# Cross entropy over 8192 rows: 128 loads of 16000 columns became 125 loads of 16384 columns that run across row ends

## The chip, the cores and the metric

The kernel runs on one core of a Trainium2 chip. In the profile's words ACT is the Scalar engine, DVE the Vector engine, POOL GpSimd, and SP the engine that issues the loads. The DMA engines carry data from HBM, the chip's memory, to SBUF, the core's own memory. The metric is the device time of one execution in microseconds (us). The experiments were run in four batches on different chips, each with runs of the kernel before in the same rounds; unless it says otherwise, a difference is taken against those. The profile's span is about 1.7 us shorter than the device time of the same execution; I compare device times with device times and spans with spans.

## The reference, cut to what matters

```python
# logits: (16, 512, 32000) float32, labels: (16, 512) integer
logits_max = np.max(logits, axis=-1, keepdims=True)
log_sum_exp = np.log(np.sum(np.exp(logits - logits_max), axis=-1)) + logits_max.squeeze(-1)
loss = log_sum_exp - logits[label of the row]        # shortened
```

There are 8192 rows of 32000 float32 values, 1048.58 MB, each read once. The output has 8192 numbers. The kernel leaves the maximum out: the data are normal draws, so exp does not overflow.

## The kernel before

Each of the 128 partitions owns 64 consecutive rows, which stand as one contiguous run of 64 x 32000 values in HBM. Three SBUF buffers of 16000 columns take the loads in turn. ACT computes exp in place and sums as it goes (`accum_out`). 64 indirect gathers on POOL, one for each row of a partition, fetch the labels' logits. A tail of shrinking loads keeps the work after the last landing short.

```python
W = 16000
lg_pg = lg.rearrange("(p g) v -> p g v", g=G)          # P = 128, G = 64, V = 32000
...
plan(0, [[4000, 4000, 8000], [16000]], [(0, 0), (0, 1), (0, 2), (1, 0)])
for g in range(1, G - 2):
    plan(g, [[W], [W]], [(0, 0), (1, 0)])
plan(G - 2, [[W], [10000, 6000]], [(0, 0), (1, 0), (1, 1)])
plan(G - 1, [[7400, 5840, 2260], [4540, 3720, 2920, 1780, 1460, 1120], [960]], ...)
...
data = ctx.enter_context(tc.tile_pool(name="data", bufs=3))
sums = persist.tile([P, G - 1, 5], FP32)
...
for g in range(G):
    nc.gpsimd.indirect_dma_start(out=lab_logit[:, g:g + 1], ..., in_=lg,
        in_offset=bass.IndirectOffsetOnAxis(ap=idx[:, g:g + 1], axis=1))
...
def exp(g, ap):
    ...
    nc.scalar.activation(out=ap, in_=ap, func=EXP, accum_out=s)

for j, (g, b, at, n) in enumerate(loads):
    ...
    nc.sync.dma_start(out=t[:, at:at + n], in_=lg_pg[:, g, c0:c0 + n])
    exp(g, t[:, at:at + n])
```

The softmax here doesn't subtract the row's maximum and nothing guards it: scores larger than these inputs give would overflow.

## Time and profile before

| | before |
|---|---|
| device time | 2435.71 us median of 3 (2435.50 to 2435.98) |
| bytes read | 1048.67 MB, 431 GB/s over the span |
| ACT busy | 72% of the span |
| loads, exps | 139, 139 |
| one full load, steady | 18.90 us (three in 56.70 us) |
| exp of one full load | 13.54 us |

These lines are from the page of the kernel before. The engine line has busy time, share of the span and instructions. The DMA line has the busy tenths of the 16 DMA engines in 40 equal slices. The queue lines have packets, MB and share of the engines' time. The last line is the chain that ended last.

```profile
span 2434.1 us, 807 instructions
DVE 1.3 (0%) x5; ACT 1748.9 (72%) x281; POOL 61.0 (3%) x70
DMA  9999999999999999999999999999999999999998
...
q1 hardware_dynamic: 20304, 1048.62, 99.8%
...
q14 instruction: 6, 0.05, 0.0%
...
DMA t<-in_logits_dram 76%; ACT t L105 24%; SPq L113 0%; ACTq L105 0%; ACT logsum_last L127 0%; DVE res_last L128 0%; ACT logsum L120 0%
```

The DMA engines are full from end to end. The chain's 24% of ACT does not mean that ACT holds up a quarter of the time. The same chain in order of time (start, duration, what) shows why:

```profile
1137.65 42.97 DMA t<-in_logits_dram
...
1180.70 13.64 ACT t L105 x2
1194.35 43.65 DMA t<-in_logits_dram
...
1238.08 13.64 ACT t L105 x2
1251.73 42.96 DMA t<-in_logits_dram
...
1294.78 13.64 ACT t L105 x2
```

With three buffers, the end of an exp releases the load three places later, and that load lands behind two others that were already queued. The step "exp 13.64, DMA 42.96" is therefore three loads long: 56.70 us for three loads of 8.192 MB, 18.90 us each, 433.4 GB/s. The Trainium skill, "DMA: Bandwidth & Descriptors", section "Where 436 GB/s comes from", puts the ceiling of the SBUF ports at 435.2 GB/s, and this trace comes to 99.6% of it.

The groups by shape (busy us, mean ns | idle before, releaser) give the price of an exp: 0.833 ns per column from the two shapes, and about 0.20 us that does not depend on the width.

```profile
L105 ACT ACTIVATE t<-t 128x16000 f32<-128x16000 f32 x124 | 1678.5, 13536 | 666.4 <-DMA t<-in_logits_dram 666.4
...
L105 ACT ACTIVATE t<-t 128x8000 f32<-128x8000 f32 x1 | 6.9, 6869 | 6.4 <-DMA t<-in_logits_dram 6.4
```

### The profile page before, as it was taken

To read this page: it belongs to the slowest core of one execution; us is meant where nothing else is said; L and a number is where in the kernel's file an instruction comes from. 1 tells how busy PE (TensorE), PEld (TensorE's weight loads), DVE (VectorE), ACT (ScalarE), POOL (GpSimd) and SP (SyncE) were. 2 spreads that over 40 slices of the span, in tenths; PEclk is the share of its full clock that TensorE was granted. 3 is DMA by queue.
4 is the path that set the end of the run, shared out by engine and by line. 5 is a ranking of instruction groups with operands and counts; after the bars stand their busy time and mean duration, and the time that the engine had idled before them with its cause. 6 is when DMAs were issued, how large, how long until landed. Compare 5 with 4: busy or idle time off the path is not lost.

```text
span 2434.1 us, 807 instructions
## 1 busy us (share of the span) xinstructions
DVE 1.3 (0%) x5; ACT 1748.9 (72%) x281; POOL 61.0 (3%) x70
## 2 busy tenths in 40 slices
DVE  0000000000000000000000000000000000000000
ACT  4777766777677776777677776777667776777769
POOL 3222000000000000000000000000000000000000
DMA  9999999999999999999999999999999999999998
GB/s 421 422 421 433 425 438 431 427 438 438 433 426 436 438 434 426 435 438 434 426 435 436 435 430 431 436 435 430 431 436 438 431 427 436 438 433 426 438 433 377
DMA packets 22502, 1048.77 MB, mean 431 GB/s; under 512 B 4576, under 2 KB 4704, under 8 KB 5216
## 3 DMA queue, kind: packets, MB, share of 16 engines
q1 hardware_dynamic: 20304, 1048.62, 99.8%
q0 software_dynamic: 2048, 0.04, 0.1%
q10 hardware_dynamic: 144, 0.07, 0.0%
q14 instruction: 6, 0.05, 0.0%
HBM read 1048.67 MB, written 0.03 MB: 431 GB/s over the span
## 4 chain that ended last, share of the span: by engine, by line
DMA 76%; ACT 24%; issue 0%; SPq 0%; ACTq 0%; DVE 0%
DMA t<-in_logits_dram 76%; ACT t L105 24%; SPq L113 0%; ACTq L105 0%; ACT logsum_last L127 0%; DVE res_last L128 0%; ACT logsum L120 0%
## 5 line engine op out<-in xcount | busy, mean ns | idle before, releaser
L105 ACT ACTIVATE t<-t 128x16000 f32<-128x16000 f32 (+5 forms) x139 | 1734.8, 12481 | 681.4 <-DMA t<-in_logits_dram 681.2
L89 POOL DMA_INDIRECT lab_logit<-in_logits_dram,idx x64 | 60.3, 942 | 178.3 <-DMA lab_logit<-in_logits_dram,idx 174.5
L105 ACT ACTIVATION_READ_ACCUMULATOR t<-t 128x1 f32 x139 | 25.9, 186 | 0.0
L84 ACT ACT_TABLE_LOAD x1 | 1.3, 1283 | 1.2 <-PEq L144 1.2
L118 DVE TENSOR_REDUCE totals<-sums 128x63 f32<-128x315 f32 x1 | 0.5, 480 | 2398.9 <-ACT t L105 2398.9
L87 POOL TENSOR_TENSOR idx<-idx,labs 128x64 int32<-128x64 int32 x1 | 0.3, 322 | 7.5 <-DMA labs<-in_labels_dram 7.5
L85 DVE MEMSET sums<- 128x315 f32 x1 | 0.3, 321 | 0.9 <-PEq L144 0.9
L127 ACT ACTIVATE logsum_last<-sums_last,part 128x1 f32<-128x1 f32 x1 | 0.3, 294 | 0.0
L121 DVE TENSOR_TENSOR res<-logsum,lab_logit 128x63 f32<-128x63 f32 x1 | 0.2, 225 | 25.3 <-ACT logsum L120 25.3
L120 ACT ACTIVATE logsum<-totals 128x63 f32<-128x63 f32 x1 | 0.2, 238 | 0.0
L86 POOL IOTA idx<- 128x64 int32 x1 | 0.2, 172 | 0.4 <-PEq L155 0.4
L123 DVE TENSOR_REDUCE part<-sums_last 128x1 f32<-128x9 f32 x1 | 0.2, 163 | 4.0 <-ACT t L105 4.0
L128 DVE TENSOR_TENSOR res_last<-logsum_last,lab_logit 128x1 f32<-128x1 f32 x1 | 0.2, 159 | 1.2 <-ACT logsum_last L127 1.2
L144 POOL MEMSET const-uint8-127<- 128x1 uint8 x1 | 0.1, 118 | 0.0
L144 POOL MEMSET const-bfloat16-1.0<- 128x1 bf16 x1 | 0.1, 113 | 0.0
L144 POOL MEMSET const-float32-0.0<- 128x1 f32 x1 | 0.1, 98 | 0.2 <-issue 0.2
L144 POOL MEMSET const-float32-1.0<- 128x1 f32 x1 | 0.1, 104 | 0.0
## 6 DMA issues: line engine op xcount, KB each, us to landing
t<-in_logits_dram SPq DMA_DIRECT2D x124, 8000.0 KB, 43.0
t<-in_logits_dram SPq DMA_DIRECT2D x1, 5000.0 KB, 35.9
t<-in_logits_dram SPq DMA_DIRECT2D x2, 2000.0 KB, 9.6
t<-in_logits_dram SPq DMA_DIRECT2D x1, 4000.0 KB, 21.4
t<-in_logits_dram SPq DMA_DIRECT2D x1, 3700.0 KB, 32.9
t<-in_logits_dram SPq DMA_DIRECT2D x1, 3000.0 KB, 42.6
t<-in_logits_dram SPq DMA_DIRECT2D x1, 2920.0 KB, 39.5
t<-in_logits_dram SPq DMA_DIRECT2D x1, 2270.0 KB, 26.4
```

Source lines behind the costliest of these rows:

```text
L84: nc.scalar.preload_act_table_set("natural_log_exp_and_others")
L85: nc.vector.memset(sums[:], 0.0)
L86: nc.gpsimd.iota(idx[:], pattern=[[V, G]], base=0, channel_multiplier=G * V)
L87: nc.gpsimd.tensor_tensor(out=idx[:], in0=idx[:], in1=labs32, op=ALU.add)
L89: nc.gpsimd.indirect_dma_start(out=lab_logit[:, g:g + 1], out_offset=None, in_=lg, in_offset=bass.IndirectOffsetOnAxis(ap=idx[:, g:g + 1], ...
L105: nc.scalar.activation(out=ap, in_=ap, func=EXP, accum_out=s)
L118: nc.vector.reduce_sum(out=totals[:], in_=sums[:], axis=X)
L120: nc.scalar.activation(out=logsum[:], in_=totals[:], func=LN)
L121: nc.vector.tensor_tensor(out=res[:], in0=logsum[:], in1=lab_logit[:, 0:G - 1], op=ALU.subtract)
L123: nc.vector.reduce_sum(out=part[:], in_=sums_last[:, 0:K - 1], axis=X)
L127: nc.scalar.activation(out=logsum_last[:], in_=sums_last[:, K - 1:K], func=LN, bias=part[:])
L144: nc = _bacc.Bacc("TRN2", target_bir_lowering=False, num_devices=1)
```

## The change

The intent: fewer, larger transfers. A partition's 64 rows are contiguous, so they can be loaded as one run of 125 pieces of 16384 columns (65536 B). A piece then crosses row ends, and its exp has to be cut there so that every row's sum stays its own: 63 row ends inside pieces, 199 exps in place of 139.

```diff
-    W = 16000
+    W = 16384
-    lg_pg = lg.rearrange("(p g) v -> p g v", g=G)
+    lg_p = lg.rearrange("(p g) v -> p (g v)", g=G)
...
-    plan(0, [[4000, 4000, 8000], [16000]], [(0, 0), (0, 1), (0, 2), (1, 0)])
-    for g in range(1, G - 2):
-        plan(g, [[W], [W]], [(0, 0), (1, 0)])
-    plan(G - 2, [[W], [10000, 6000]], [(0, 0), (1, 0), (1, 1)])
+    plan([[4096, 4096, 8192]], [(0, 0), (0, 1), (0, 2)])
+    for _ in range(G * V // W - 4):
+        plan([[W]], [(0, 0)])
+    plan([[10000, 6384]], [(0, 0), (0, 1)])
     plan(
-        G - 1,
-        [[7400, 5840, 2260], [4540, 3720, 2920, 1780, 1460, 1120], [960]],
+        [[8168, 5840, 2260], [4540, 3720, 2920, 1780, 1460, 1120], [960]],
...
-    for j, (g, b, at, n) in enumerate(loads):
+    done = 0
+    for j, (b, at, n) in enumerate(loads):
...
-        nc.sync.dma_start(out=t[:, at:at + n], in_=lg_pg[:, g, c0:c0 + n])
-        exp(g, t[:, at:at + n])
+        nc.sync.dma_start(out=t[:, at:at + n], in_=lg_p[:, done:done + n])
+        end = done + n
+        while done < end:
+            g = done // V
+            m = min(end, (g + 1) * V) - done
+            exp(g, t[:, at:at + m])
+            done += m
+            at += m
```

More of the change, by code (lines that the diff above doesn't have):

```diff
@@ L43, with plan @@
     loads = []
-    def plan(g, widths_by_buffer, order):
-        n_buffers = 1 + max((l[1] for l in loads), default=-1)
+    def plan(widths_by_buffer, order):
+        n_buffers = 1 + max((l[0] for l in loads), default=-1)
         for b, i in order:
             ws = widths_by_buffer[b]
-            loads.append((g, n_buffers + b, sum(ws[:i]), ws[i]))
-    plan(0, [[4000, 4000, 8000], [16000]], [(0, 0), (0, 1), (0, 2), (1, 0)])
-    for g in range(1, G - 2):
-        plan(g, [[W], [W]], [(0, 0), (1, 0)])
-    plan(G - 2, [[W], [10000, 6000]], [(0, 0), (1, 0), (1, 1)])
+            loads.append((n_buffers + b, sum(ws[:i]), ws[i]))
+    plan([[4096, 4096, 8192]], [(0, 0), (0, 1), (0, 2)])
+    for _ in range(G * V // W - 4):
+        plan([[W]], [(0, 0)])
+    plan([[10000, 6384]], [(0, 0), (0, 1)])
     plan(
-        G - 1,
-        [[7400, 5840, 2260], [4540, 3720, 2920, 1780, 1460, 1120], [960]],
+        [[8168, 5840, 2260], [4540, 3720, 2920, 1780, 1460, 1120], [960]],
         [(0, 0), (0, 1), (1, 0), (1, 1), (1, 2), (0, 2), (1, 3), (1, 4), (1, 5), (2, 0)],
     )
-    assert sum(l[3] for l in loads) == G * V
+    assert sum(l[2] for l in loads) == G * V
     data = ctx.enter_context(tc.tile_pool(name="data", bufs=3))
@@ L97 @@
     buffers = {}
-    col = {}
     n_exp = {}
@@ L110 @@
         t = buffers[b]
-        c0 = col.get(g, 0)
-        col[g] = c0 + n
-        nc.sync.dma_start(out=t[:, at:at + n], in_=lg_pg[:, g, c0:c0 + n])
-        exp(g, t[:, at:at + n])
+        nc.sync.dma_start(out=t[:, at:at + n], in_=lg_p[:, done:done + n])
[6 more added lines that the diff above has]
+            at += m
         left = len(loads) - 1 - j
```

## The prediction

> **What bounds the kernel now.** The loads. The page has the 16 DMA engines at 9 tenths in 39 of 40 slices, 431 GB/s over the span. The chain that ended last is 76% DMA and 24% exp, but the exp share comes from how the chain is walked: with three buffers a load is issued by the exp three loads back, and lands behind two loads already queued. In order of time the chain repeats 13.64 us exp, 42.96 us DMA, every 56.70 us for three loads: 18.90 us per 8.192 MB load, 433.4 GB/s. The Trainium skill, "DMA: Bandwidth & Descriptors", section "Where 436 GB/s comes from", gives 435.2 GB/s as the ceiling of the SBUF ports; the trace agrees (99.6% of it). ACT is 72% busy and waits 5.27 us for the load before each full exp. 1048.58 MB at 435.2 GB/s is already 2409 us (estimate from that section).
>
> **What the change does.** Bytes: unchanged. Full pieces go from 64000 to 65536 B per partition, 8 descriptors per engine and load. Median durations in the trace's DMA records: 2366 ns for 64000 B, 1185 ns for 32000 B, so about 4 ns are fixed per descriptor (estimate), or 13 ns if the ceiling's rate is the slope. The equivalent of three full loads fewer saves 24 descriptors per engine: 0.1 to 0.3 us. A new load should take 18.90 x 16384/16000 = 19.35 us.
>
> ACT: 199 exps for 139 (63 row ends fall inside pieces). The groups by shape give 13.536 us for 16000 columns and 6.869 us for 8000: 0.833 ns per column plus 0.20 us; each accumulator read adds 0.19 us, half of it hidden. +60 x about 0.3 = +18 us, to about 1766 us busy. The worst piece with one split takes 14.2 us against a load of 19.35 us: 5 us still idle, all off the critical path. Buffers come free 0.5 us later, with over 24 us of loads still queued: the DMA never runs dry.
>
> Start: first pieces of 4096 for 4000, DMA bound either way. The 64 gathers beside the first 290 us cost the stream the same. Tail: the same last-row exps but for 768 columns of row 62 in front, 0.9 us, which eats the 0.3 to 0.5 us waits of the tail's first exps and is nearly caught up by the 3720-column piece: 0 to +0.3 us.
>
> **Sum.** -0.3 to +0.3 us: 2435.6 us, range 2431 to 2442. Within 2%: 0.95; faster 0.01; slower 0.04.
>
> **What would show it.** Chain: 58.05 us per three loads, about 14 us of it exp; a load's issue-to-landing 44 us for 43.0. ACT busy 1766 us, 199 exps, still waiting 5 us for the DMA before each full one. Packets of 65536 B and 2.42 us. Mean still 431 GB/s.
>
> **What would make it wrong.** (a) A 64 KiB piece might be cut in two descriptors: 4 ns x 8 x 125 = +4 us; a finer cut costs more. (b) Every piece now starts on a 64 KiB boundary of its partition's run. The same page, section "Latency and other measured facts", reports lower rates at large power-of-two row pitches in HBM; but the pitch between partitions (8,192,000 B = 125 x 64 KiB) stays, and this trace shows no loss at it, so I expect none. (c) Three 64 KiB buffers stand at a power-of-two pitch in SBUF; ACT might be slowed, but it has 5 us a piece to give.

## The result, and the profile after

| | before | after |
|---|---|---|
| device time, first measurement | 2435.61 us, median of 4 (2435.34 to 2435.98) | 2436.14 us, median of 4 (2436.03 to 2436.36) |
| ratio | | 1.0002, 95% interval 0.9985 to 1.002 |
| ACT busy | 1748.9 us | 1759.5 us |
| full load, steady | 18.90 us | 19.35 us, for 1.024 times the bytes |
| instruction packets (queue 14) | 6 | 7 |

A ratio here is the mean time of one kernel's runs over that of the other's of the same rounds, so it is not quite the ratio of the medians quoted. The ranges of the two kernels do not overlap: the change is half a microsecond slower, 0.02%.

The page of the changed kernel, the lines that answer to those above:

```profile
span 2434.5 us, 867 instructions
DVE 1.4 (0%) x5; ACT 1759.5 (72%) x401; POOL 61.2 (3%) x70
DMA  9999999999999999999999999999999999999998
...
q1 hardware_dynamic: 19872, 1048.62, 99.8%
...
q14 instruction: 7, 0.06, 0.0%
...
DMA t<-in_logits_dram 75%; ACT t L104 24%; SPq L111 0%; ACTq L104 0%; ACT logsum_last L131 0%; DVE res_last L132 0%; ACT logsum L124 0%
```

The load queue has 432 packets fewer, ACT has 120 instructions more (60 exps, each with an instruction that reads the accumulator), and the DMA engines are as full as they were. The chain in order of time:

```profile
1441.37 13.96 ACT t L104 x2
1455.34 44.00 DMA t<-in_logits_dram
...
1499.42 14.14 ACT t L104 x4
1513.58 44.48 DMA t<-in_logits_dram
...
1558.14 13.96 ACT t L104 x2
1572.11 44.00 DMA t<-in_logits_dram
...
1616.20 14.14 ACT t L104 x4
...
1630.36 43.81 DMA t<-in_logits_dram
```

From 1441.37 to 1499.42 three loads take 58.05 us. The piece with a cut ("x4": two exps and two reads) needs 14.14 us and the piece without 13.96 us, so a cut costs ACT 0.18 us, and the DMA stretch behind it is as much shorter (43.81 us in the last line, 44.00 us without a cut): the time does not see it. The groups by shape:

```profile
L104 ACT ACTIVATE t<-t 128x16384 f32<-128x16384 f32 x59 | 817.5, 13856 | 312.8 <-DMA t<-in_logits_dram 312.8
```

312.8 us of idle time over 59 exps is 5.3 us before each full exp, waiting for the load, as before. The duration of 13.856 us is the old 13.536 us plus 384 columns at 0.833 ns: the buffers at a 64 KiB pitch do not slow ACT.

One stretch stands out: 44.48 us where the pattern has 43.8 us (after a piece with a cut) or 44.0 us (after one without). I took each landing's lag behind a steady pace of 18.90 us per 16000 columns from the timelines. Outside the first 300 us and the tail the lag is flat to 0.1 us but for steps of 0.5 to 0.7 us: two of them before (near 1200 and 2010 us), three after (near 920, 1560 and 2160 us).

### The profile page after: what moved, and what is told of

It reads as the page before. It is cut to its first block, busy times and chain, and to the rows that moved or that the text cites. A ratio compares the mean times of both kernels' runs of the same rounds, so it can differ in the third digit from the quotient of the medians.

```text
span 2434.5 us, 867 instructions
## 1 busy us (share of the span) xinstructions
DVE 1.4 (0%) x5; ACT 1759.5 (72%) x401; POOL 61.2 (3%) x70
## 4 chain that ended last, share of the span: by engine, by line
DMA 75%; ACT 24%; issue 0%; SPq 0%; ACTq 0%; DVE 0%
DMA t<-in_logits_dram 75%; ACT t L104 24%; SPq L111 0%; ACTq L104 0%; ACT logsum_last L131 0%; DVE res_last L132 0%; ACT logsum L124 0%
## 5 line engine op out<-in xcount | busy, mean ns | idle before, releaser
L104 ACT ACTIVATE t<-t 128x16384 f32<-128x16384 f32 (+33 forms) x199 | 1745.8, 8773 | 670.9 <-DMA t<-in_logits_dram 670.7
L104 ACT ACTIVATION_READ_ACCUMULATOR t<-t 128x1 f32 x199 | 37.1, 186 | 0.0
```

## The experiments

The theory: the loads bound the time at the pace of bytes, and the added exps disappear in ACT's idle time. The rival: two effects of some 10 us cancel (60 cuts at 0.18 us are 11 us of work; the wide loads might give as much back). Two more theories came up on the way. Theory B, from the steps just told: more instructions cost time through the DMA engines, because the instructions themselves are fetched by DMA. Theory C, from the runs that tested B: the packets of one consumer (an engine whose instructions they carry) run on one DMA engine, and the load stream follows whichever DMA engine is furthest behind. (Theory A in the expectations is the first one, "exps in idle time cost nothing at all".)

| run | us, median | before, same rounds | instruction packets | what it tells |
|---|---|---|---|---|
| change again | 2436.22 | 2435.86 | 7 | +0.36 |
| wide loads, uncut exps | 2435.69 | 2435.86 | 6 | -0.17, inside the scatter |
| narrow loads, cut exps | 2436.57 | 2435.86 | 7 | +0.71 |
| change, off 64 KiB | 2436.48 | 2435.86 | 8 | alignment: nothing |
| change, off 256 B | 2436.16 | 2435.79 | 7 | alignment: nothing |
| exps cut in 16 (kernel before) | 2456.45 | 2435.79 | 35 | +20.66 with ACT still waiting |
| 1280 memsets on DVE | 2443.13 | 2435.79 | 16 | +7.34, nothing else changed |
| change, loads cut in 4 | 2464.61 | 2435.79 | 11 | the price of a descriptor |
| change, no gathers | 2431.27 | 2435.79 | 6 | the gathers cost 5 us (against the change, 2436.22) |
| 40 exps cut in 50 | 2566.79 | 2435.79 | 37 | where ACT stops being hidden |
| 1280 memsets on POOL | 2441.06 | 2435.90 | 16 | +5.16 for the same 10 packets |
| 1280 memsets on DVE and on POOL | 2443.69 | 2435.90 | 26 | +7.79 for 20 packets: they do not add |

### The change again

No edit: the changed kernel on the chip of the next three runs.

> The changed kernel unaltered, on the chip of the three runs beside it. Theory (the loads bound the time, the added exps hide in ACT's idle time): the same as before within 1 us, and where the first measurement had +0.5 us (2436.14 against 2435.61) this one shows whether that is more than scatter between profiles: +0.0 to +0.8 us. Rival (two effects of 10 us or so that cancel: 60 added exps cost 60 x 0.18 = 11 us, wide loads give them back): also the same; this run doesn't tell them apart, the next two do.

Measured: 2436.22 us (2435.91 to 2436.32, 5 runs) against 2435.86 us (2435.68 to 2436.11, 9 runs). A difference of +0.36 us is there again, but the two ranges overlap.

### Wide loads alone

```diff
-        end = done + n
-        while done < end:
-            ...
-            exp(g, t[:, at:at + m])
-            ...
+        done += n
+        exp((done - 1) // V, t[:, at:at + n])
```

> Wide loads alone: the changed kernel's loads, one exp per load without the cut at row ends (wrong sums on purpose; 136 exps). Theory: 2435.3 to 2436.3 us, ACT busy down to about 1748 us, the loads' period unchanged at 19.35 us. Rival (cancelling effects): about 11 us faster than before, 2425 us.

Measured: 2435.69 us (2435.68 to 2435.89), 0.17 us under before. The ranges overlap, so the gain by itself is not shown. The rival's 2425 us is out. The sums are wrong, and the output still passed the comparison's tolerance, so "correct" says little there. ACT does the old kernel's amount of work and the instruction packets are back to 6.

### Cut exps alone

```diff
-        exp(g, t[:, at:at + n])
+        if 1 <= g <= 60 and c0 == 0:
+            exp(g, t[:, 0:8000])
+            exp(g, t[:, 8000:n])
+        else:
+            exp(g, t[:, at:at + n])
```

> Cut exps alone: the old kernel's loads of 16000 columns, with 60 of its full exps cut in two (199 exps, right result). Theory: 2435.3 to 2436.0 us, ACT busy about 1760 us, its idle time smaller by as much. Rival (cancelling effects): about 11 us slower, 2446 us.

Measured: 2436.57 us (2436.15 to 2436.67). The rival's 2446 us is out: 11 us of exps did disappear. But the theory's 2435.3 to 2436.0 us is missed as well, by 0.6 us. The cuts cost 0.71 us here, although ACT waits for the load as often as before (131 times, 670.8 us in all against 681.2 us):

```profile
ACT t L105 <- DMA t<-in_logits_dram: 670.8, 131, 12.1
...
q14 instruction: 7, 0.06, 0.0%
```

The loads, the tail and the gathers are the old kernel's; what differs is ACT's program, 120 instructions longer, and one more packet on the instruction queue. Its landings have three steps of about 0.7 us where the old kernel has two.

The trace's records of single DMA packets show what a step is. From the kernel before, start in us by the records' own clock, bytes, ns (the usual 64000 B descriptor takes 2366 ns at the median):

```
 736.94   8192   309   queue 14
 737.3   64000  2781   queue 1
1196.12   8192   309   queue 14
1196.4   64000  2739   queue 1
2009.47   8192   309   queue 14
2009.8   64000  2739   queue 1
```

An instruction packet holds a DMA engine for 0.31 us, and the load's descriptor that starts as it ends is 0.37 us (0.42 us at 737 us) longer than usual: together 0.68 us, the size of the step. The packet at 737 us lengthened its descriptor too, but made no step in the landings; theory C below takes that up.

### The 64 KiB boundary

```diff
-    plan([[4096, 4096, 8192]], [(0, 0), (0, 1), (0, 2)])
+    plan([[4000, 4000]], [(0, 0), (0, 1)])
...
+    plan([[8384]], [(0, 0)])
     plan([[10000, 6384]], [(0, 0), (0, 1)])
```

> The changed kernel with 121 of its 16384-column pieces started at 8000 columns (32000 B past a 64 KiB boundary) in place of on the boundary; descriptors stay 65536 B, and the 8384 columns left over are one load before the tail. Theory (no cost in the alignment): within 1 us of the changed kernel, packets at 2422 ns. Rival (64 KiB starts in HBM cost something that hides in the sum): faster than the changed kernel by over 1 us, packets shorter than 2422 ns.

Measured: 2436.48 us (2436.07 to 2436.74), packets of 65536 B at 2422 ns as in the changed kernel. Where pieces start against 64 KiB boundaries has no effect here, neither way.

### 32 bytes past a multiple of 256

The same edit with `[[4000, 4008]]` and `[[8376]]`.

> As the run off the 64 KiB boundary, but pieces start at 8008 columns, 32032 B past the boundary, which is 32 B past a multiple of 256 B. If only the 64 KiB boundary is without meaning: the Trainium skill's page on DMA, section on how a descriptor splits into AXI transactions, has a descriptor that does not start 256 B aligned read from the 256 B boundary below it, one transaction more. At 8 to 9 ns each (256 B at 27 B per ns, estimate from this trace's descriptors) 121 x 8 descriptors are +8 us: 2444 us, packets at 2431 ns. If the read side hides it behind the write: 2436 us, packets at 2422 ns.

Measured: 2436.16 us (2436.01 to 2436.39), packets again at 2422 ns. If there is one more read transaction per descriptor, it does not show at this size of descriptor.

### Many small exps, ACT still hidden

```diff
-        exp(g, t[:, at:at + n])
+        for i in range(N if n == W else 1):                 # N = 16, sums widened to 2 * N
+            m = n // N if n == W else n
+            exp(g, t[:, at + i * m:at + (i + 1) * m])
```

> The old kernel with each of its 124 full exps cut into 16 of 1000 columns (1860 more exps, right result). By the 0.18 us that a cut cost in the two profiles ACT needs about 13.54 + 15 x 0.18 = 16.2 us per load of 18.90 us, so it stays hidden. Theory A (exps in idle time cost nothing at all): 2435.5 to 2436.5 us. Theory B (they cost through the DMA engines: each 8192 B packet of the instruction queue delayed the load stream by 0.66 us in the traces so far, and 60 more exps brought one more such packet): 15 to 30 more instruction packets and +0.66 us for each, so 2445 to 2456 us, with ACT still waiting for every load.

Measured: 2456.45 us (2456.24 to 2456.71), +20.66 us, 0.45 us above theory B's range, which had 0.66 us for a packet. From the page, the waits and the groups by shape of this run:

```profile
span 2454.9 us, 4528 instructions
DVE 4.5 (0%) x5; ACT 2092.4 (85%) x4001; POOL 61.4 (3%) x70
...
q14 instruction: 35, 0.29, 0.0%
```

```profile
ACT t L106 <- DMA t<-in_logits_dram: 358.7, 127, 12.2
```

```profile
L106 ACT ACTIVATE t<-t 128x1000 f32<-128x1000 f32 x1984 | 2022.5, 1020 | 345.4 <-DMA t<-in_logits_dram 345.4
```

ACT waited for the loads 127 times, 358.7 us in all, so it is not the bound: 16 exps of 1.02 us are 16.3 us against 18.90 us. There are 29 instruction packets more, and 20.66 / 29 = 0.71 us for each. The count fits too: 1860 exps with 1860 accumulator reads are 3720 instructions, 128 for each of 29 packets, and 8192 / 128 is 64 B per instruction. Theory A ("exps in idle time cost nothing at all") is out.

### Instructions on an engine that does nothing

```diff
     nc.vector.memset(sums[:], 0.0)
+    spare = persist.tile([P, 1], FP32)
+    for _ in range(1280):
+        nc.vector.memset(spare[:], 0.0)
```

> The old kernel with 1280 one-column memsets on the otherwise idle DVE at its start (right result); ACT's and SP's programs are as before. Theory A: 2435.5 to 2436.5 us. Theory B (instruction packets delay the loads, whichever engine they feed): 1280 instructions at 64 B (estimate: 60 more exps with their accumulator reads are 120 instructions and came with one 8192 B packet, so 60 to 128 instructions a packet) are 10 to 21 more packets, so +6.6 to +14 us at 0.66 us each.

Measured: 2443.13 us (2443.08 to 2443.20), +7.34 us.

```profile
span 2441.3 us, 2086 instructions
DVE 76.8 (3%) x1285; ACT 1748.8 (72%) x281; POOL 61.4 (3%) x70
...
q14 instruction: 16, 0.13, 0.0%
```

ACT's busy time is the old kernel's to 0.1 us, and nothing waits for these memsets. 1280 / 128 = 10 packets more, and 7.34 / 10 = 0.73 us for each. This separates the instruction packets from everything that the cut exps do on ACT. That 0.73 us is so near ACT's 0.71 us is luck, though. In this run's records the load descriptor behind a DVE packet is 0.65 to 0.71 us longer than usual, in place of 0.37 us, so such a packet takes about 1.0 us of its DMA engine, and at 500 us the loads are 8.7 us later than in the old kernel. The end is only 7.34 us later because the old kernel's two steps of 0.67 us, near 1200 and 2010 us, do not come here. Why DVE's packets cost more is open; it is not the gathers beside them, because ACT's packet at 65 us in the run with 16 exps a load, among the same gathers, has the usual 0.37 us.

One thing did not fit a fixed price for each packet. From 300 us to the tail this run's landings have no step at all, though its records have instruction packets near 1205 and 2016 us like the old kernel's. The stretch that took 43.65 us at 1194 us before is now

```profile
1146.29 42.96 DMA t<-in_logits_dram
...
1202.98 42.96 DMA t<-in_logits_dram
```

So a packet can cost nothing even while the DMA engines are full. I linked the records from 300 us on into sequences, each descriptor to the one that starts within some 10 ns of its end. In the old kernel that gives 16 sequences of 880 to 884, as 16 DMA engines should. The instruction packets fall on two of them: those at 382.7, 1196.1 and 2009.5 us on one, those at 736.9 and 1947.2 us on another, and only the first sequence's packets made steps. In the changed kernel (run again) those at 313.1, 933.0, 1552.9 and 2153.5 us are on one sequence and the one at 910.4 us on another. That suggested theory C: each load lands when its slowest DMA engine is done, so only packets on the DMA engine that is furthest behind count. The next two runs tested it.

### The same on POOL, and on both

```diff
     # after the gathers
+    spare_p = persist.tile([P, 1], FP32)
+    for _ in range(1280):
+        nc.gpsimd.memset(spare_p[:], 0.0)
```

The second run has these and the DVE memsets of the run before.

> The old kernel with 1280 one-column memsets on POOL after its gathers, from about 290 us on (right result). The control for the next run: 10 more instruction packets. Theory C (each consumer's packets run on one DMA engine of its own, and the load stream follows the DMA engine that is furthest behind): about 10 x 0.68 us less the 1.35 us of the two later steps of the old trace, which are then hidden, so +4.5 to +6.8 us, 2440.3 to 2442.6 us, and the steps near 1200 and 2010 us are gone. Theory B (each packet costs 0.7 us wherever it falls): +6.6 to +7.3 us, 2442.4 to 2443.1 us, steps still there.

> The old kernel with both: 1280 memsets on DVE at the start and 1280 on POOL after the gathers, 20 more instruction packets (right result). Theory B (each packet costs 0.7 us): +14 us, 2450 us. Theory C (one DMA engine for each consumer, the one furthest behind counts): DVE's DMA engine stays the one furthest behind, so hardly more than with DVE alone (+7.3 us): 2443 to 2444.5 us, and no step in the landings after 160 us.

Measured: 2441.06 us (2440.86 to 2441.17) with POOL alone, +5.16 us, and 2443.69 us (2443.36 to 2443.84) with both, +7.79 us. Theory B's 2442.4 to 2443.1 us and 2450 us are missed, theory C's ranges hold.

```profile
span 2442.0 us, 3366 instructions
DVE 76.8 (3%) x1285; ACT 1748.8 (72%) x281; POOL 188.0 (8%) x1350
...
q14 instruction: 26, 0.21, 0.0%
```

20 packets more than the old kernel cost nearly what DVE's 10 cost alone (7.34 us): POOL's 10, worth 5.16 us by themselves, add 0.45 us (the two runs with DVE are from different batches). Each of the two runs' landings is flat to 0.1 us from 500 us to the tail, without the old steps near 1200 and 2010 us. The stretch at 1194 us of the old kernel (43.65 us) reads in the run with both:

```profile
1203.53 42.96 DMA t<-in_logits_dram
```

The linked sequences show theory C at work. I compared when each of the 16 completes the same load, by its 4-byte completion records, as a distance behind the median of the 16:

| run | sequence with | before -> after its packet(s) | furthest behind of the others | landings |
|---|---|---|---|---|
| before | ACT's at 1185 us | 0.68 -> 1.37 us | 0.60 us | step of 0.67 us |
| before | SP's at 1936 us | 0.54 -> 1.26 us | 1.38 us | no step |
| DVE | ACT's at 1194 us | 0.68 -> 1.36 us | 9.35 us | no step |
| POOL | POOL's ten | up to 7.37 us | 0.9 us | +6.7 us |
| both | POOL's eight after 300 us | 2.13 -> 7.37 us | 10.04 us | no step |

(Times are from the span's start. The names ACT and SP are inferred from how often the packets come: every 43 and every 64 loads. The 9.35 and 10.04 us are one sequence in the runs with DVE's memsets; it is taken for DVE's.) Every packet here sets its own sequence back by about 0.7 us, and the loads follow only when that sequence is the last. This also tells why ACT's packet at 371 us (382.7 us by the records' clock) made no step: it brought its sequence to 0.66 us behind, where another already was at 0.64 us.

### The price of a descriptor

```diff
-        nc.sync.dma_start(out=t[:, at:at + n], in_=lg_p[:, done:done + n])
+        q = n // 4 if n == W else n
+        for i in range(0, n, q):
+            nc.sync.dma_start(out=t[:, at + i:at + i + q], in_=lg_p[:, done + i:done + i + q])
```

> The changed kernel with each of its 121 full loads issued as four of 4096 columns into the same buffer, exps as they were (right result). 24 more data descriptors per engine and full load, 2904 in all, and 363 more DMAs. Settles the cost of a descriptor that the prediction had at 4 or 13 ns: +12 us at 4 ns, +38 us at 13 ns, +55 us at the 19 ns that the steady periods of the two traces give (0.45 us for 24 descriptors); plus 3 us for 363 more semaphore descriptors of 9 ns, plus 2 to 4 us for some 3 to 6 more instruction packets. Expected by the steady periods: about 2490 us; by the descriptor durations alone: about 2452 us.

Measured: 2464.61 us (2464.47 to 2465.02), nearer to the low expectation of 2452 us than to 2490 us. The chain in order of time goes from landing to landing of two pieces here:

```profile
910.38 39.14 DMA t<-in_logits_dram
...
949.53 39.14 DMA t<-in_logits_dram
```

949.53 - 910.38 = 39.15 us is 19.57 us for a piece of 16384 columns against 19.35 us in one DMA: 0.22 us for 24 more data descriptors per engine, about 9 ns each, the three added completion descriptors included. So 24 descriptors fewer in the whole change are worth about 0.2 us, and the steady periods' 19 ns had been too high. 121 pieces at 0.22 us are 26.6 us of the +28.4 us over the change (2464.61 - 2436.22, another batch's median); the run also has 4 more instruction packets.

### Without the gathers

```diff
-    for g in range(G):
-        nc.gpsimd.indirect_dma_start(...)
+    nc.vector.memset(lab_logit[:], 0.0)
```

> The changed kernel without its 64 indirect gathers (labels' logits set to 0, wrong result on purpose). The loads' landings lag the steady pace by a further 4.5 us over the first 290 us in both traces; if the gathers do that, 2430 to 2432 us here, the landings on the steady pace from the first full load, and fewer instruction packets. If the lag is start-up, 2436 us. Both theories of the change expect the first.

Measured: 2431.27 us (2431.20 to 2431.38), with one instruction packet fewer; the output is wrong. The landings are on the steady pace from the first full load. So the gathers and their instructions cost 5 us of the load stream (2436.22 - 2431.27, another batch's median) in the changed kernel. The old kernel was not run without them; its landings lag the steady pace as much over the first 300 us (at 300 us 8.8 us against 9.1 us, and 4.0 us without gathers).

### Where ACT stops being hidden

```diff
+        m = 320 if 10 <= g < 30 else n
-        exp(g, t[:, at:at + n])
+        for i in range(0, n, m):
+            exp(g, t[:, at + i:at + i + m])     # the row's accumulators are overwritten: wrong result
```

> The old kernel with the 40 full exps of rows 10 to 29 cut into 50 of 320 columns (1960 more exps; the row's accumulators are overwritten, wrong result on purpose). By the cut exps of 1000 columns, one start to the next is 0.833 us per 1000 columns plus 0.185 us, so 50 x 0.452 = 22.6 us per load against 18.90 us: ACT is over the load's period for these 40 loads alone. Theory (time is the longer of the two per load, hidden below it and not above): ACT back to back for 40 x 22.6 = 905 us in which 41 loads of 18.90 us = 775 us pass, so +130 us, 2566 us, within 10; about 30 more instruction packets, which now fall into DMA idle time and add nothing. Rival (each instruction packet costs 0.7 us wherever it falls): 2587 us.

Measured: 2566.79 us (2566.59 to 2566.96). The first theory's 2566 us holds. The chain, and the group by shape:

```profile
516.81 44.98 ACT t L105 x200
...
561.99 44.97 ACT t L105 x200
```

```profile
L105 ACT ACTIVATE t<-t 128x320 f32<-128x320 f32 x2000 | 903.6, 453 | 5.3 <-DMA t<-in_logits_dram 5.3
```

Two loads' exps take 561.99 - 516.81 = 45.18 us, 22.6 us per load against a load of 18.90 us, and ACT is back to back. There are 31 instruction packets more, about as many as the 29 of the run with 16 exps a load, yet the 22 us of the rival are not there: the time is the one that was expected if the packets fall into the idle time of DMA engines that wait for ACT.

No version came out of this that is worth having: the wide loads gain about 0.2 us at best, and the 60 cuts that make them correct cost an instruction packet of 0.7 us.

## Why the prediction was right

The time (2436.14 us against 2435.6 us, range 2431 to 2442) and the verdict were right, and so was the mechanism that carried them. The prediction's own sum, -0.3 to +0.3 us, was missed by a little: +0.53 us and, again, +0.36 us. The last point of this list is the term that it lacked.

- "Bound by the loads": right. A cut of 0.18 us on ACT leaves the period of three loads at 58.05 us, the predicted number; issue to landing has a median of 44.0 us, packets take 2.42 us, the mean is 431 GB/s. With ACT loaded to 16.3 us per load the exps stayed hidden; with 22.6 us they did not.
- "24 descriptors fewer save 0.1 to 0.3 us": right. About 0.22 us by the cut loads (9 ns each, between the 4 and the 13 ns of the prediction), and -0.17 us for wide loads alone, which agrees but is inside the scatter.
- "+18 us of ACT work, 1766 us busy": the direction was right, the size was not. It measured +10.6 us, 1759.5 us. The mis-sized term is "x about 0.3": a cut costs 0.18 us. The accumulator read starts 0.09 us before its exp ends and the rest of it runs under the next exp, so none of its 0.19 us shows between two exps, and the half that was added to the 0.20 us was too much. It was off the critical path and cost the prediction nothing.
- "Tail 0 to +0.3 us": the last exp starts 0.17 us later, but not for the reason given. These lines are from the timeline before, then after (start, duration, engine, and in brackets the wait):

```profile
2417.28 3.30 ACT L105 ACTIVATE t<-t 128x3720 f32<-128x3720 f32 x1 [0.33 <-DMA t<-in_logits_dram]
...
2430.02 1.00 ACT L105 ACTIVATE t<-t 128x960 f32<-128x960 f32 x1
```

```profile
2417.46 3.30 ACT L104 ACTIVATE t<-t 128x3720 f32<-128x3720 f32 x1 [0.30 <-DMA t<-in_logits_dram]
...
2430.19 1.00 ACT L104 ACTIVATE t<-t 128x960 f32<-128x960 f32 x1
```

  ACT had caught up with the extra exp and waited for the 3720-column piece in both kernels. The piece itself landed 0.18 us later. The span is 0.36 us longer in this pair of profiles: the rest comes after the last output DMA was issued (2431.66 and 2431.84 us), and no run explains it.
- "(a) a piece cut in two descriptors, (b) 64 KiB starts, (c) buffer pitch": none came true. 15488 packets of 65536 B are 121 loads x 128 partitions, one descriptor each; two shifts of the start changed nothing; the exp of 16384 columns has the expected duration.
- Missing altogether: exps in idle time are not free. They are instructions, 128 of them are one packet of 8192 B, and a packet of ACT's on the DMA engine that is furthest behind takes about 0.7 us out of a saturated load stream. The changed kernel has one such packet more, and three steps in its landings for two: +0.7 us, less the 0.2 us of the descriptors, which agrees with the +0.4 to +0.5 us measured. That the omission did no harm is due to the small number of cuts: with 1860 more exps it would have been a 20 us error.

What stays open: the records name no DMA engine. The sequences that I linked by time are an inference, and two DMA engines that end within a few ns of each other could be swapped in them. Which engine's instructions travel on which DMA engine is inferred too, what the packets before 300 us cost in the old kernel is hidden by the gathers, and why DVE's packets cost about 1.0 us no run tells. The +0.36 us and +0.53 us are also close to the scatter of one kernel's runs. Of their two parts, the packet is clear in the runs that multiply it, and the descriptors in the run with cut loads.

## What to carry to other kernels

When the DMA engines are full for the whole span and the pace is within a per cent of the ceiling, as here, widening transfers that are already 64000 B per partition buys only the descriptors saved: count them and multiply by a few nanoseconds (about 9 here) before writing the change. Work added to an engine that waits for loads stayed hidden while its time per load was below the load's (16.3 us against 18.90 us, but not 22.6 us). Its instructions still travel through the DMA engines, so in a DMA-bound kernel a long unrolled program, even on an idle engine, can have a price: here 0.7 us (ACT, POOL) to 1.0 us (DVE) for 128 instructions when their packets are on the DMA engine that is furthest behind, and close to nothing otherwise. A small stretch that breaks the pattern in the chain of waits deserves a look: two of them, 0.7 us each, were in the old trace before anything was run.

## What the Trainium skill lacked or had wrong

- "Runtime: NRT & Kernel Launch", section "Instruction fetch mechanics", has the refills in blocks of 16 KiB (256 instructions) and calls the cost of crossing a block one that is mostly hidden. Here they show as packets of 8192 B, 128 instructions of 64 B each (29 packets for 3720 instructions, 10 for 1280), and with saturated DMA engines they cost 0.71 and 0.73 us each at the end of those two runs (the second is about 1.0 us at the packet, less what it hides). They were hidden in the run bound by ACT (31 packets, no cost seen) and where another consumer's packets had already put a DMA engine further behind (10 packets for 0.45 us). No page says that second thing of instruction packets.
- "DMA: Bandwidth & Descriptors", section "Why small descriptors are slow (HBM only)", has about 3 cycles per packet and 32 B of metadata per operation, but no time for a large descriptor in a saturated stream: about 9 ns beyond its bytes here (0.22 us for 24 and their 3 completion descriptors), at 16384 B against 65536 B. The page has none for indirect gathers beside such a stream: 64 gathers of 128 elements and their instructions cost 5 us.
- The same page, section "How a descriptor splits into AXI transactions", has one more transaction for a descriptor that does not start on a multiple of 256 B. At 65536 B per descriptor that did not show: 2422 ns both ways, 2436.16 us against 2436.22 us (two batches; +0.37 and +0.36 us over their own kernel before).
- "ScalarE: Activation LUTs", section "What ACT_TABLE_LOAD costs", has 186 ns + 0.833 ns per column for an ACTIVATE and 93 ns of overlap between two in a row; no page has what the accumulator's read adds. Here an exp with an accumulated sum takes 0.833 ns per column plus 0.185 us from one start to the next, the read included (320 columns: 0.452 us), so the two exps do not overlap; that the read between them takes up the 93 ns is argued, because no run has exps without it.
